# The low part of every second weight piece: an accumulating DMA in place of a VectorE subtraction

## The chip, the cores and the metric

The kernel runs on one core of one Trainium2 chip. The metric is device time in microseconds (us). Three runs of the kernel before took 2153.18, 2155.61 and 2155.78 us; their median is 2155.61 us.

## What is computed

Two layers of an encoder over 256 tokens of width 2048, in float32. Cut to what matters, a layer is

```
h   = RMSNorm(x);  p = h @ W_in                    # 2048 x 4624
A   = windowed attention;  M = mLSTM, both ways    # from the columns of p
x   = x + RMSNorm(concat(A, M) @ W_out)            # 2048 x 2048
x   = x + RMSNorm(relu(RMSNorm(x) @ W_up)^2 @ W_down)   # 2048 x 8192, 8192 x 2048
```

Nearly all the work is in the four products with the weights. The weights are 378 MB, read from HBM once.

## The kernel before

**Precision.** Each float32 operand of a product is split in two float32r parts: the high part is the operand rounded (written by ScalarE as a plain copy), the low part is the operand minus the high part. A product is then three matmuls: high by high, high by low, low by high. In the up projection the weights are the stationary operand and the moving operand holds both parts of the tokens, so two matmuls, of 512 and 256 columns, do the same.

**Tiles and pieces.** The weights are cut in column tiles, taken in the order of use: per layer 10 of the input projection (two of them narrow, 272 and 256 columns, the others 512), 4 of the output projection, and 4 blocks of 4 up tiles and 4 down tiles. That is 92 tiles in all. `load` (printed below) brings a tile in as four pieces q = 0..3, each [128, 4, 512] floats (1 MB), or [128, 16, 128] where the weights are stationary. For each piece SyncE's queue issues a DMA from `wall` in HBM to a buffer `raw` (L185), ScalarE writes the high part `whi` (L186), VectorE the low part `wlo` (L187). Of `raw` there are 2 buffers, of `whi` and `wlo` 4 each, all taken in turn. So the load of a piece waits until the piece two before it has been read out of `raw`, and the split of a piece waits until TensorE has ended with the piece four before it.

**Order.** `mm_tile` (L198 to L200 are its three matmuls) and `mm_stationary` (L266, L269) load their own tile and the one behind it, then issue the products. Work beside the products (attention, mLSTM, evacuation of PSUM) is emitted between them. Norms end on a chain over ScalarE (sums of squares, L309), VectorE and GpSimd (a power, L293 as `y_ro`, `y_rd`, `y_s`), then the residual (L788), transposes on TensorE (L328) and a split of the transposed tokens (`h2T`, `hT`: high part by ScalarE, L320, low part by GpSimd, L321). A scheduler sets each engine's order from a simulated time line. Each engine runs its own instructions in that order, so an instruction that waits holds up those behind it.

The first tile of all is loaded with a `begin` function in smaller steps; all others without.

Of the kernel before, what the change touches and what calls it, by code (L numbers as in the profile page):

```python
# [20 lines left out]
DM = 2048  # L21
# [22 lines left out]
# Column tiles of the input projection, in the order in which they are multiplied.  # L44
# [14 lines left out]
PK = 4  # contraction chunks in one weight piece  # L59
# [3 lines left out]
def _stage_widths():  # L63
    """Per layer: (stage, block, tile, width) in the order of use."""
    out = [("in", 0, j, w) for j, w in enumerate(IN_W)]
    out += [("out", 0, n, 512) for n in range(4)]
    for b in range(4):
        out += [("up", b, n, 512) for n in range(4)]
        out += [("down", b, n, 512) for n in range(4)]
    return out  # L70
# [5 lines left out]
def stationary(key):  # L76
    """Whether a column tile's weights are the stationary operand: the up projection's but for
    each layer's first, which starts on one token tile alone."""
    _, st, b, n = key
    return st == "up" and (b, n) != (0, 0)  # L80
# [6 lines left out]
def encoder_kernel(ctx, tc, x, wall, rope, conv_w, gate_bias, ml_g, sink, gpre, gpost, out):  # L87
# [14 lines left out]
    # ---------------------------------------------------------------- constants  # L102
# [15 lines left out]
    # column before row; column after row  # L118
# [24 lines left out]
    # rows split in two parts, the second NG2 further on, and what adds the two of one row  # L143
# [9 lines left out]
    # ---------------------------------------------------------------- weights  # L153
# [12 lines left out]
    def load(i, begin=None):  # L166
        """Load and split one column tile: four pieces, each [128, 4, w] of 512 rows, or, where
        the weights are stationary, [128, 16, 128] of 128 columns. begin(q) precedes piece q."""
        if i >= len(order) or order[i] in pieces:
            return  # L170
        o, w = offs[order[i]]
        k, n = (KC, P) if stationary(order[i]) else (PK, w)
        got = []
        for q in range(NPC):
            raw = wraw.tile([P, k, n], F32, tag="raw", name="raw")
            a = o + q * P * k * n
            src = wall[a:a + P * k * n].rearrange("(p k n) -> p k n", p=P, k=k)
            if begin is not None:
                begin(q)
            hi = wsp.tile([P, k, n], F32R, tag="hi", name="whi")  # L180
            lo = wsp.tile([P, k, n], F32R, tag="lo", name="wlo")
            step = 1 if begin is not None and q < 2 else k
            for j in range(0, k, step):
                sl = slice(j, j + step)
                nc.sync.dma_start(raw[:, sl], src[:, sl])  # L185
                nc.scalar.activation(hi[:, sl], raw[:, sl], AF.Copy)  # L186
                nc.vector.tensor_tensor(out=lo[:, sl], in0=raw[:, sl], in1=hi[:, sl].bitcast(F32), op=ALU.subtract)  # L187
            got.append((hi, lo))
        pieces[order[i]] = got
# [12 lines left out]
    # Work beside the products, emitted in small steps between them: `urgent` empties PSUM.  # L202
# [12 lines left out]
    def mm_tile(key, T, stages=(), after=None, at=None, half=False):  # L215
        """One column tile for both token tiles, in PSUM tiles for each. `stages`: (first, last)
        contraction chunks in which token tile 0 runs ahead of token tile 1; after(t, ps) is called
        behind each token tile's last product, at[t, k]() before a staged product. `half`: all work
        beside ends before the second half of the contraction."""
        load(pos[key])  # L220
        load(pos[key] + 1)
        if stages:
            ps = [psmm.tile([P, NT, 512], F32, tag="mm", name="mm")[:, 0] for _ in range(NT)]
        else:
            both = psmm.tile([P, NT, 512], F32, tag="mm", name="mm")
            ps = [both[:, t] for t in range(NT)]
        stages = list(stages)
        ended = []
        k = 0
        while k < KC:  # L230
            if stages and k == stages[0][0]:
                first, k = stages.pop(0)
                for t in range(NT):
                    for i in range(first, k):
                        if at is not None and (t, i) in at:
                            at[t, i]()
                        mm_k(ps[t], key, T, i, t)
                    if after is not None and k == KC:
                        after(t, ps[t])
                        ended.append(t)  # L240
                continue
            if half and k == KC // 2:
                while pump():
                    pass
            for t in range(NT):
                mm_k(ps[t], key, T, k, t)
            pump()
            k += 1
        if after is not None and not ended:
            for t in range(NT):  # L250
                after(t, ps[t])
        return ps

    def mm_stationary(key, T, after):
        """The transposed product of one column tile: weights stationary, both halves of the
        transposed tokens moving. after(pair, ps) gets two chunks of columns: [128, 2, 512] with
        the products of the tokens' upper and lower halves, to be added."""
# [15 lines left out]
    # ---------------------------------------------------------------- norms  # L273
    def rsq(ss, n, div, name):
        """(mean of squares + eps) ** -0.5 for n independent sums."""
# [12 lines left out]
    def rsq_row(part, last, name):  # L288
        """part: (sum of squares of the first columns) / DM + eps; last: the last columns' sum."""
# [33 lines left out]
    def pre(t, n, T, norm, eng=None):  # L323
        """512 columns of x of one token tile transposed, times the norm's gain, split."""
# [12 lines left out]
    def pre_scale(t, name):  # L337
        """The norm's scale of x of one token tile."""
        ss = small.tile([P, 4], F32, tag="ss", name=f"ss_{name}")
        for n in range(4):  # L340
            square_sum(xs[:, t, n * 512:(n + 1) * 512], ss[:, n:n + 1])
        return rsq_row(rsq_part(ss[:, :3], name), ss[:, 3:4], f"{name}{t}")

    # ---------------------------------------------------------------- attention
    def rope_half(ps, t, c0, nh, s):
        """Rotary on nh heads at columns c0.. of a product's tile; scaled by s."""
# [15 lines left out]
    SLACK = 3  # steps left for other engines  # L362
    ASC = float(HD) ** -0.5

    def attend(pair, qT, kT, vA, nsink, snk, attT):
        """Two heads of one group: heads 2*pair and 2*pair + 1."""
# [3 lines left out]
        for t in range(NT):  # L370
# [5 lines left out]
            # keys out of the window: beyond it for the first query tile, before it for the second  # L376
# [40 lines left out]
    # ---------------------------------------------------------------- mLSTM  # L417
    CF = 0.25 * float(HD) ** -0.5
    DIRS = ((0, 0, 1), (32, 1, 0))  # first row, first chunk, second chunk

    def gates(gp, cols):
        """gp [128, chunk, 16] -> rows of the scans, and columns in cols [128, 6, NG]:
        source exponents by chunk, end weights by chunk, floors by chunk."""
# [9 lines left out]
        # log1p(e) = 2 atanh(e / (2 + e)), by its series to beyond float32  # L433
# [41 lines left out]
        for r0, c1, c2 in DIRS:  # L475
# [4 lines left out]
            # running maximum behind the first chunk, in its own frame and in the next one's  # L480
# [23 lines left out]
    def conv_silu(zp, cw, dst):  # L504
        """Centred convolution over tokens and silu, times 2, of one chunk of channels."""
# [10 lines left out]
    def qk_heads(ps, c0, heads, s, cw, qk):  # L516
        """q and k columns of some heads from c0 on: transposed, convolved, activated."""
# [18 lines left out]
    def mlstm_head(h, qk, va, cols, hm, hr, name):  # L536
        """Both directions summed, into hm[:, h] [128, chunk, 256]; and its norm's scale, into hr."""
        # weights of sources for targets, transposed: [s, direction, t]
# [28 lines left out]
        # state behind each direction's first chunk, and q weighted for it  # L567
# [42 lines left out]
    def gate_in(h, ps, c0, sh, mg):  # L610
        """tanh of half of a head's gate; with it the sigmoid is (tanh + 1) / 2."""
        for t in range(NT):
            nc.scalar.activation(mg[:, h % 2, t], ps[t][:, c0:c0 + DV], AF.Tanh, scale=sh[t])

    def gate_mul(h, mg, hm, hr, gated):
        """A head normalised and gated, times 2."""
# [8 lines left out]
    def gate_out(h, hm, mlc, memT):  # L625
        """A gated head transposed, times its gain; split."""
# [11 lines left out]
    # ---------------------------------------------------------------- layers  # L638
# [16 lines left out]
    def pre_at(t, k, tp, T, norm):  # L655
        """Token tile tp's transposes within a staged tile, from token tile t's product k on."""
        return {(t, k + i): (lambda i=i: pre(tp, i, T, norm)) for i in range(4)}

    for l in range(DEPTH):
# [77 lines left out]
        # input projection  # L737
# [43 lines left out]
        # output projection, residual, next norm  # L781
# [37 lines left out]
        # MLP  # L819
# [87 lines left out]
def _pieces(w, cols=None):  # L907
    """[K, n] -> contiguous pieces [K / 512][128, 4, n], flat."""
# [47 lines left out]
```

## Time and profile before

| | |
|---|---|
| median of three runs | 2155.61 us |
| span of the profiled execution, first to last instruction | 2154.7 us |
| TensorE busy | 2118.5 us, 98% of the span |
| VectorE busy | 1211.4 us, 56% |
| ScalarE busy | 939.4 us, 44% |
| GpSimd busy | 60.9 us, 3% |
| moved by DMA | 388.13 MB, 51% of the 16 DMA engines' time |

The profiled execution has no time beside its span. The span lies 0.9 us under the median of the runs, inside their spread of 2.6 us. Busy time counts each engine by itself; that they overlap is read from the waits and the time line. TensorE's granted clock was 0.997 of its full 2.4 GHz.

### The profile page before, as it was taken

The numbers are of one execution on the slowest core, as the hardware profiler recorded it, in microseconds if no ns is written. First come the engines' busy times: TensorE is split into PE (matmuls) and PEld (weight loads), VectorE is DVE, ScalarE is ACT, GpSimd is POOL, SyncE is SP. The second block draws the span as 40 slices with busy tenths as digits, with TensorE's granted clock in tenths as the row PEclk, the third lists the DMA queues.
The fourth block names the chain that finished last, engine by engine and source line by source line (L and its number), as shares of the span: only waits on it lengthen the run. The fifth ranks groups of instructions, "written<-read, shape, count | busy, mean of one in ns | idle before, by whom it ended". The sixth has DMA issues, their size and how long they took to land.

```text
span 2154.7 us, 25194 instructions
## 1 busy us (share of the span) xinstructions
PE 2118.5 (98%) x10492; PEld 1779.7 (83%) x10492; DVE 1211.4 (56%) x1339; ACT 939.4 (44%) x1017; POOL 60.9 (3%) x68
## 2 busy tenths in 40 slices
PE   8999999999999999999999999999999999999998
PEld 6878887888888888888878788878888888888886
DVE  6656566654554555555576656565445545545554
ACT  5445545443443343344354554454434434433432
POOL 0000002000000000000020000030000000000000
PEclk9999999999999999999999999999999999999999
DMA  7434354555555555555554344546555555555553
GB/s 250 165 137 176 120 198 171 195 195 187 184 193 188 187 194 183 188 195 186 181 181 156 134 153 149 203 149 213 187 188 193 184 190 193 184 189 194 186 192 116
DMA packets 62195, 388.13 MB, mean 180 GB/s; under 512 B 9600, under 2 KB 10112, under 8 KB 17280
## 3 DMA queue, kind: packets, MB, share of 16 engines
q1 hardware_dynamic: 61936, 386.48, 51.2%
q8 instruction: 82, 1.34, 0.2%
q14 instruction: 33, 0.27, 0.0%
q10 hardware_dynamic: 144, 0.03, 0.0%
HBM read 384.39 MB, written 2.10 MB: 179 GB/s over the span
## 4 chain that ended last, share of the span: by engine, by line
PE 94%; DVE 2%; DMA 2%; ACT 1%; POOL 1%; issue 1%; POOLq 0%; DVEq 0%; SPq 0%; ACTq 0%
PE mms L266 21%; PE mm L200 19%; PE mm L199 19%; PE mm L198 19%; PE mms L269 11%; DMA raw<-wall 1%; PE sc L374 1%; PE pn L590 1%; PE po L413 1%; DVE xs L788 1%; POOL h2T L321 1%; DVE wlo L187 0%; ACT whi L186 0%; PE cp L573 0%; PE pn L593 0%
## 5 line engine op out<-in xcount | busy, mean ns | idle before, releaser
L187 DVE TENSOR_TENSOR wlo<-raw,whi 128x2048 fp32r<-128x2048 f32 (+3 forms) x374 | 828.8, 2217 | 811.2 <-ACT whi L186 810.7
L186 ACT ACTIVATE whi<-raw 128x2048 fp32r<-128x2048 f32 (+3 forms) x374 | 692.9, 1853 | 984.0 <-PE mm L200 537.8
L266 PE MATMUL mms<-h2T,whi 128*128 128x512 f32 x1920 | 678.8, 397 | 0.0
L269 PE MATMUL mms<-h2T,wlo 128*128 128x256 f32 x1920 | 539.7, 281 | 0.0
L266 PEld LDWEIGHTS mms<-h2T,whi 128*128 128x128 f32 x1920 | 361.0, 188 | 88.9
L200 PE MATMUL mm<-whi,uT 128*128 128x512 f32 x1024 | 403.1, 394 | 0.0
L199 PE MATMUL mm<-wlo,uT 128*128 128x512 f32 x1024 | 401.4, 392 | 0.0
L198 PE MATMUL mm<-whi,uT 128*128 128x512 f32 x1024 | 397.4, 388 | 0.0
L269 PEld LDWEIGHTS mms<-h2T,wlo 128*128 128x128 f32 x1920 | 360.4, 188 | 0.3
L198 PE MATMUL mm<-whi,hT 128*128 128x512 f32 (+2 forms) x640 | 241.8, 378 | 7.2 <-ACT hT L320 5.1
L200 PE MATMUL mm<-whi,hT 128*128 128x512 f32 (+2 forms) x640 | 241.6, 378 | 1.5 <-POOL hT L321 1.4
L199 PE MATMUL mm<-wlo,hT 128*128 128x512 f32 (+2 forms) x640 | 240.7, 376 | 0.0
L199 PEld LDWEIGHTS mm<-wlo,uT 128*128 128x128 f32 x1024 | 192.2, 188 | 44.7
L198 PEld LDWEIGHTS mm<-whi,uT 128*128 128x128 f32 x1024 | 192.2, 188 | 43.0
L200 PEld LDWEIGHTS mm<-whi,uT 128*128 128x128 f32 x1024 | 192.5, 188 | 38.3
L198 PEld LDWEIGHTS mm<-whi,hT 128*128 128x128 f32 x640 | 121.1, 189 | 28.0 <-ACT hT L320 5.7
L200 PEld LDWEIGHTS mm<-whi,hT 128*128 128x128 f32 x640 | 121.1, 189 | 23.2 <-POOL hT L321 2.2
L199 PEld LDWEIGHTS mm<-wlo,hT 128*128 128x128 f32 x640 | 121.0, 189 | 20.3 <-DVE wlo L187 0.2
L866 DVE SCALAR_TENSOR_TENSOR A_mlp<-mm,s2q,A_mlp 128x512 f32<-128x512 f32 x48 | 34.0, 746 | 37.9 <-PE mm L200 37.9
L198 PE MATMUL mm<-whi,memT 128*128 128x512 f32 x128 | 50.9, 398 | 0.0
L199 PE MATMUL mm<-wlo,attT 128*128 128x512 f32 x128 | 50.7, 396 | 0.0
L198 PE MATMUL mm<-whi,attT 128*128 128x512 f32 x128 | 50.6, 395 | 0.0
(220 smaller groups left out, 1403.4 us busy)
## 6 DMA issues: line engine op xcount, KB each, us to landing
raw<-wall SPq DMA_DIRECT2D x350, 1024.0 KB, 4.8
raw<-wall SPq DMA_DIRECT2D x8, 544.0 KB, 3.6
g<-gpost SPq DMA_DIRECT2D x16, 256.0 KB, 4.3
raw<-wall SPq DMA_DIRECT2D x8, 512.0 KB, 3.4
xs<-x_in SPq DMA_DIRECT2D x8, 256.0 KB, 5.3
raw<-wall SPq DMA_DIRECT2D x8, 256.0 KB, 6.7
y_out<-xs SPq DMA_DIRECT2D x8, 256.0 KB, 2.8
cossin<-rope SPq DMA_DIRECT2D x1, 256.0 KB, 7.7
```

Source lines behind the costliest of these rows:

```text
L186: nc.scalar.activation(hi[:, sl], raw[:, sl], AF.Copy)
L187: nc.vector.tensor_tensor(out=lo[:, sl], in0=raw[:, sl], in1=hi[:, sl].bitcast(F32), op=ALU.subtract)
L198: nc.tensor.matmul(dst, lhsT=xh, rhs=hi, start=(k == 0), stop=False)
L199: nc.tensor.matmul(dst, lhsT=xh, rhs=lo, start=False, stop=False)
L200: nc.tensor.matmul(dst, lhsT=xl, rhs=hi, start=False, stop=(k == KC - 1))
L266: nc.tensor.matmul(ps[:, i], lhsT=hi[:, k], rhs=Tk.rearrange("p j t -> p (j t)"), start=(k == 0), stop=False)
L269: nc.tensor.matmul(ps[:, i, :SEQ], lhsT=lo[:, k], rhs=Tk[:, 0], start=False, stop=(k == KC - 1))
L321: (eng or nc.vector).tensor_tensor(out=lo, in0=ps, in1=hi.bitcast(F32), op=ALU.subtract)
L374: nc.tensor.matmul(sc[:, j], lhsT=qT[:, q0 + j, t * P:(t + 1) * P], rhs=kT[:, g], start=(j == 0), stop=False)
L413: nc.tensor.matmul(po[:, j], lhsT=vA[:, kb, g * HD:(g + 1) * HD], rhs=pT[:, kb], start=(kb == 0), stop=(kb == 1))
L590: nc.tensor.matmul(pn[:, :DV + 1], lhsT=dt[:, d, c], rhs=va[:, c, h], start=True, stop=(c == c1))
L866: nc.vector.scalar_tensor_tensor(out=acc[:, t, sl], in0=ps, scalar=s2[t], in1=acc[:, t, sl], op0=ALU.mult, op1=ALU.add)
```

## The change

In every tile but the first, the pieces q = 1 and q = 3 are formed in another way. ScalarE writes minus the high part into `wlo` (a copy with scale -1). GpSimd's queue then issues a DMA that reads the same piece of `wall` from HBM once more and adds it onto `wlo`. ScalarE writes the high part into `whi` as before. VectorE has no part in these pieces. Nothing else changes; in the rest of the diff comments are taken out.

```diff
             for j in range(0, k, step):
                 sl = slice(j, j + step)
                 nc.sync.dma_start(raw[:, sl], src[:, sl])
+                if begin is None and q % 2 == 1:
+                    nc.scalar.activation(lo[:, sl], raw[:, sl], AF.Copy, scale=-1.0)
+                    nc.gpsimd.dma_start(lo[:, sl], src[:, sl], accum_op=ALU.add)
+                    nc.scalar.activation(hi[:, sl], raw[:, sl], AF.Copy)
+                    continue
                 nc.scalar.activation(hi[:, sl], raw[:, sl], AF.Copy)
                 nc.vector.tensor_tensor(out=lo[:, sl], in0=raw[:, sl], in1=hi[:, sl].bitcast(F32), op=ALU.subtract)
```

That concerns 182 pieces: 174 of 1 MB, 4 of 544 KB and 4 of 512 KB (the narrow tiles). In the changed kernel the lines behind the new ones stand 5 further on; L187 is minus the high part, L188 the DMA, L189 the high part of an odd piece, L191 and L192 the split of an even one.

ScalarE's order in the first down block of layer 0, before (`A_mlp` is the block's sum, which ScalarE writes behind each tile of this block; `uz` and `uT` are the up projection's evacuation and split in the block behind it):

```order
L186 ACTIVATE whi<-raw 128x2048 x4
L864 ACTIVATE A_mlp<-mm,s2q 128x512 x2
L186 ACTIVATE whi<-raw 128x2048 x4
L864 ACTIVATE A_mlp<-mm,s2q 128x512 x2
L186 ACTIVATE whi<-raw 128x2048 x2
L844 ACTIVATE uz<-mms 128x512
```

and at the same place in the changed kernel:

```order
L869 ACTIVATE A_mlp<-mm,s2q 128x512 x2
L191 ACTIVATE whi<-raw 128x2048
L187 ACTIVATE wlo<-raw 128x2048
L189 ACTIVATE whi<-raw 128x2048
L191 ACTIVATE whi<-raw 128x2048
L187 ACTIVATE wlo<-raw 128x2048
L189 ACTIVATE whi<-raw 128x2048
L869 ACTIVATE A_mlp<-mm,s2q 128x512 x2
L191 ACTIVATE whi<-raw 128x2048
L189 ACTIVATE whi<-raw 128x2048
L187 ACTIVATE wlo<-raw 128x2048
L849 ACTIVATE uz<-mms 128x512
```

Every second piece has two ScalarE instructions that read `raw`; in the down tiles minus the high part comes first, in the up tiles second.

GpSimd's order from the output projection to the first up tile of layer 0, before:

```order
L293 TENSOR_TENSOR y_ro_2869<-v_ro_2867,nhalf 128x1
L321 TENSOR_TENSOR h2T_2877<-xg,h2T_2877 128x4x128 x2
L321 TENSOR_TENSOR h2T_2878<-xg,h2T_2878 128x4x128 x2
L293 TENSOR_TENSOR y_ro_2959<-v_ro_2957,nhalf 128x1
```

and there in the changed kernel:

```order
L188 DMA wlo<-wall 128x2048 x6
L298 TENSOR_TENSOR y_ro_2897<-v_ro_2895,nhalf 128x1
L188 DMA wlo<-wall 128x2048
L298 TENSOR_TENSOR y_ro_2987<-v_ro_2985,nhalf 128x1
L326 TENSOR_TENSOR h2T_2905<-xg,h2T_2905 128x4x128
L188 DMA wlo<-wall 128x2048
L298 TENSOR_TENSOR y_s_3204<-v_s_3202,nhalf 128x1
L326 TENSOR_TENSOR h2T_2905<-xg,h2T_2905 128x4x128
L326 TENSOR_TENSOR h2T_2906<-xg,h2T_2906 128x4x128 x2
```

The power for the second token tile (`y_ro`) now stands ahead of the token split, and an accumulating DMA stands between the first and the second of the four splits of token tile 0.

## Rows read from the trace of the kernel before

**Rows 1.** The page's first part: busy time, share, instructions of each engine.
```profile
PE 2118.5 (98%) x10492; PEld 1779.7 (83%) x10492; DVE 1211.4 (56%) x1339; ACT 939.4 (44%) x1017; POOL 60.9 (3%) x68
```

**Rows 2.** The chain that ended last, shares of the span by engine.
```profile
PE 94%; DVE 2%; DMA 2%; ACT 1%; POOL 1%; issue 1%; POOLq 0%; DVEq 0%; SPq 0%; ACTq 0%
```

**Rows 3.** Busy time by stage: start:end, length, then engines, clock, DMA share, GB/s.
```profile
340.00:380.00 40.00, 37.96 (x183) 30.71 (x182) 28.49 (x50) 23.05 (x38) 16.38 (x12) 1.00 0.40 145
380.00:1060.00 680.00, 680.00 (x3413) 574.36 (x3412) 360.04 (x244) 276.22 (x206) 0.00 (x0) 1.00 0.54 191
1060.00:1100.00 40.00, 35.93 (x166) 29.04 (x165) 30.70 (x56) 19.55 (x33) 15.26 (x13) 0.96 0.42 145
...
1400.00:1450.00 50.00, 47.99 (x228) 39.13 (x227) 35.31 (x54) 27.41 (x42) 16.39 (x12) 1.00 0.40 140
```

**Rows 4.** Who waited for VectorE's low parts (line L187): total us, times.
```profile
  PEld mm L199: 0.9, 3
```

**Rows 5.** Groups by line and shape: count, busy us, mean ns, idle before.
```profile
L187 DVE TENSOR_TENSOR wlo<-raw,whi 128x2048 fp32r<-128x2048 f32 x350 | 803.3, 2295 | 783.4 <-ACT whi L186 783.2
...
L186 ACT ACTIVATE whi<-raw 128x2048 fp32r<-128x2048 f32 x350 | 670.7, 1916 | 941.5 <-PE mm L200 508.4 <-PE mms L266 366.4 <-DMA raw<-wall 61.9
...
L187 DVE TENSOR_TENSOR wlo<-raw,whi 128x1088 fp32r<-128x1088 f32 x8 | 10.3, 1290 | 13.3 <-ACT whi L186 13.3
...
L186 ACT ACTIVATE whi<-raw 128x1088 fp32r<-128x1088 f32 x8 | 8.9, 1114 | 19.4 <-PE mm L200 8.0 <-issue 7.4 <-DVE ra L359 2.4
```

**Rows 6.** ScalarE's time line, up tiles: start us, us, what, idle before and releaser.
```profile
604.39 1.92 ACT L186 ACTIVATE whi<-raw 128x2048 fp32r<-128x2048 f32 x1 [3.25 <-PE mms L266]
606.21 0.61 ACT L320 ACTIVATE uT<-uz 128x512 fp32r<-128x512 f32 x1
610.04 1.92 ACT L186 ACTIVATE whi<-raw 128x2048 fp32r<-128x2048 f32 x1 [3.22 <-PE mms L266]
```

**Rows 7.** ScalarE's time line, down tiles.
```profile
643.76 1.92 ACT L186 ACTIVATE whi<-raw 128x2048 fp32r<-128x2048 f32 x1 [3.06 <-PE mm L200]
649.26 1.92 ACT L186 ACTIVATE whi<-raw 128x2048 fp32r<-128x2048 f32 x1 [3.58 <-PE mm L200]
654.75 1.92 ACT L186 ACTIVATE whi<-raw 128x2048 fp32r<-128x2048 f32 x1 [3.58 <-PE mm L200]
```

**Rows 8.** VectorE's time line there.
```profile
645.72 2.29 DVE L187 TENSOR_TENSOR wlo<-raw,whi 128x2048 fp32r<-128x2048 f32 x1 [2.60 <-ACT whi L186]
```

**Rows 9.** DMA by window 600 to 626 us, 40 slices: busy tenths, GB/s.
```profile
DMA  9920009799700093799600075999301094999000
GB/s 429 416 88 0 0 0 176 239 441 441 315 0 0 0 139 63 328 416 403 265 0 0 0 101 151 403 403 403 151 0 25 0 176 164 441 429 391 13 0 0
```

**Rows 10.** DMA issues, window 400 to 1060 us: count, KB, median us to landing.
```profile
raw<-wall SPq DMA_DIRECT2D x120, 1024.0 KB, 4.8
```

**Rows 11.** DMA queue and issues, window 5 to 35 us.
```profile
q1 hardware_dynamic: 6324, 8.62, 87.4%
...
raw<-wall SPq DMA_DIRECT2D x4, 1024.0 KB, 7.4
```

**Rows 12.** The chain in window 340 to 380 us: start us, us, what.
```profile
351.17 2.29 DVE wlo L187
353.48 5.09 DMA raw<-wall
358.66 0.41 ACT whi L186
```

**Rows 13.** TensorE's time line in a narrow tile.
```profile
99.77 0.28 PE L198 MATMUL mm<-whi,hT 128*128 128x272 f32 x1
99.89 0.29 PE L199 MATMUL mm<-wlo,hT 128*128 128x272 f32 x1
```

**Rows 14.** GpSimd's time line at the border to the MLP.
```profile
357.35 2.56 POOL L321 TENSOR_TENSOR h2T<-xg,h2T 128x512 fp32r<-128x512 f32 x2 [9.51 <-ACT h2T L320]
361.17 4.14 POOL L321 TENSOR_TENSOR h2T<-xg,h2T 128x512 fp32r<-128x512 f32 x2 [1.25 <-ACT h2T L320]
```

## The prediction, on record before the changed kernel ran

> **What bounds the kernel now.** I read the page's busy times first: TensorE works 2118.5 us of a span of 2154.7 us, VectorE 56%, ScalarE 44%, GpSimd 3% [rows 1]. The chain that ended last puts 94% of the span on TensorE and 2% on VectorE [rows 2]. So next to nothing is to be had from VectorE's time as such. The table by stage says where TensorE waits at all: not at all in the long MLP stretch (680.00 us of 680.00), and 2.04, 4.07 and 2.01 us at the three borders between stages, 8.1 us together [rows 3]. All that TensorE waited for a low part is 0.9 us [rows 4].
>
> Then I looked at how the weights keep ahead. In the MLP a piece is split the moment TensorE lets go of the piece four before it (ScalarE's idle time ends on TensorE) [rows 6, 7]. Two pieces take 2 x 5.65 = 11.30 us in the up tiles (610.04 - 604.39) and 654.75 - 643.76 = 10.99 us in the down tiles. One buffer of `raw` is used once in that time: 4.8 us from issue to landing [rows 10], 1.92 us high part [rows 7], 2.29 us low part [rows 8], together 9.0 us. The margin of this loop is 2.0 us in the down tiles. It is the narrowest resource after TensorE. The DMA engines work 0.54 of the time [rows 3], in bursts: the busy tenths of a 26 us window show some 2.6 us of 9s and 7s for a piece, and as much rest [rows 9].
>
> **What goes and what comes.** VectorE loses 174 x 2.295 + 8 x 1.29 = 410 us [rows 5], hidden beside TensorE. Worth: between 0 and the 0.9 us of waits; I take 0.
>
> ScalarE gains 174 x 1.916 + 8 x 1.114 = 342 us [rows 5] (the four narrowest pieces are priced at the row of the next wider ones). In a pair of pieces it then has 3 x 1.92 and, in the up tiles, up to 2 x 0.61 us of other work [rows 6], 7.0 of 11.30 us. It is not the bound. The odd piece's `raw` is now free after two ScalarE instructions, 3.84 us, where it was 1.92 + 2.29 = 4.21; a gain of 0.4 us in that loop.
>
> GpSimd gains 182 DMA issues. No row shows one from its queue; hidden by 97% idle time, they matter only where something is queued behind, at the borders (below).
>
> The DMA engines get 182 transfers more. Cost of one: a copy of 1 MB takes 0.54 x 11.30 / 2 = 3.05 us of all engines [rows 3, 6], and 1.0486 MB at the best slices' 441 GB/s 2.38 us [rows 9]. An accumulating one reads the piece, reads `wlo`, and writes. Lower end: one copy, 3.05 us, since the same bytes come from HBM; a gain is excluded, for nothing is taken off the queues. Upper end: three copies, 9.15 us, if the three follow each other. I take two copies, two reads with the write beside the second; that is nearest to how a plain copy, one read with its write beside it, is priced in the row. Then a pair asks for 4 x 3.05 = 12.2 us of the engines by their mean cost, or 4 x 2.38 = 9.5 us at the best rate, of 10.99 to 11.30. So the engines are nearly full, and plain loads will land later.
>
> The Trainium skill, DMA: Bandwidth & Descriptors, section on issuing engines not being separate DMA queues, says that DMAs issued from GpSimd run on the same 16 engines as SyncE's and interleave with them; this speaks against the change, and by it the new transfers cannot pass beside the loads. The Trainium skill, Collectives: The Full Stack, part 3 on the bandwidth ceiling, has a reducing transfer at half a copy's rate (32.35 against 62.28 GB/s) because the add needs two source reads; by that one transfer is 1.93 x 3.05 = 5.9 us, an estimate, and a pair 12.0 us. No run here shows either yet.
>
> What crowding does to a load the trace shows at its start: with the engines at 87.4%, 1 MB took 7.4 us to land instead of 4.8 [rows 10, 11]. The odd piece's next load is issued just when the accumulating transfer starts, so it gets the crowded value; the even one's comes 5.65 us later and mostly not. With 0.1 us for the hand-overs (0.02 from VectorE to the issue, 0.09 from landing to ScalarE) [rows 12] the odd loop takes 7.4 + 3.84 + 0.1 = 11.34 us. That is 0.35 us over the down tiles' pair and 0.04 over the up tiles'. The pairs are 60 in the stationary up tiles, 114 in the other wide tiles (57 tiles, the first left out), 8 in the narrow ones. So 114 x 0.35 + 60 x 0.04 = 42 us. Ends: 0, if loads land within 7.0 us; and if the engines are the bound at 12.2 us, 114 x 1.21 + 60 x 0.90 = 192 us.
>
> Narrow tiles: their products follow at 0.12 us [rows 13], 24 to a piece, 2.95 us, a pair in 5.9. Behind each of the four such tiles two wide pairs come at 11.34, and 2 x 5.4 = 10.9 us of lead are used up. The low part of an odd piece had 3 x 5.5 = 16.5 us between its buffer coming free and its use; 3.84 of ScalarE and 7.4 or more of transfer leave some 5. At worst 6 to 8 us of waiting each, 32 in all; but the narrow pieces load in half the time, and the trace shows no wait there before. Between 0 and 32 us I take 3 each, 12.
>
> Borders: ahead of three of the four token splits of token tile 0 stands an accumulating DMA that waits for minus the high part of the up tile's last piece, and this for the last product of the output projection's. Before, those splits ran at 357 to 365 us as soon as ScalarE was ready [rows 14]. At the three borders I take one ScalarE instruction each, 1.92, together 6 us. Ends: 0, and 3 x (1.92 + 4.8) = 20 us, if GpSimd is held for as long as a load takes.
>
> Sum against the profiled span: 42 + 12 + 6 = 60 us on 2154.7. The median of the runs lies 0.9 us above the span, so 2155.6 + 60 = 2216 us, 2.8% slower.
>
> **The rivals.** First, the accumulating transfer costs about one copy: 9.2 us of the engines per pair, loads land soon after 4.8 us, the odd loop is 8.7 to 10 us and hides under TensorE; then 2156 us, at most 4 more from the borders. For it: the rests in the bursts, 2.6 us per piece [rows 9], hold just one such transfer. Against it: two sources.
>
> Second, it costs three copies or more: a pair needs 5 x 2.38 = 11.9 to 5 x 3.05 = 15.2 us, every odd low part comes late and TensorE waits for it everywhere. The price is 140 to 723 us, 2296 to 2880, the middle 2590. For it: nothing in this trace bounds an adding transfer from above. Against it: the bytes alone ask for two.
>
> Third, on the other side: at the borders VectorE's low part of 2.29 us stands in the chain ahead of the next load [rows 12]; without it norms and residuals end sooner and TensorE waits less. It decides if transfers cost one copy and GpSimd's splits aren't held. At most 8.1 + 0.9 us [rows 3, 4], 2147; at half of it 2151. Against it: ScalarE's added instructions stand in the same chain.
>
> That the change does not do what it says I rule out: the order shows the DMAs and VectorE's instructions gone.
>
> **How the numbers follow.** About 0.2%, 4.3 us, is what a measurement of this kernel tells from no change. Forecast (slower by waits at odd pieces, two copies) 0.52, with its own range 2162 to 2360; one copy 0.24; three copies 0.15; faster 0.09. That gives faster 0.09, same 0.24, slower 0.67. The range 2150 to 2420 us leaves out most of the faster case and two thirds of the three-copies case, 0.19.
>
> **What would show it.** Right: TensorE waits for `wlo` from the DMA, spread over the MLP, more in down than in up tiles; 1 MB loads landing at 7 us or later; DMA share near 0.9 or above with HBM bytes up by 187 MB; VectorE's group L192 at half its count. The first rival would show a DMA share near 0.8, loads near 5 us and TensorE still without a wait in the MLP. The second would show an accumulating transfer of over 9 us and pairs well over 12 us. The third would show the three borders shorter. The forecast is wrong in its main term if the time is lost at the borders or narrow tiles, or if TensorE's waits end on GpSimd's queue and not on transfers.

## The result, and the profile after

The changed kernel takes 2418.67 us (median of four runs, 2415.33 to 2431.04) against 2154.76 us before (four runs, 2153.18 to 2155.78): 1.1231 times as long, 95% interval 1.1213 to 1.1249. It is 264 us slower. The forecast was 60 us slower, with a range of its own up to 2360 us, which the time exceeds; it lies at the far end of the wide range, 2150 to 2420.

The page's first part (busy us, share of the span of 2419.2 us, instructions) and its DMA queues (packets, MB, share of 16 engines):

```profile
PE 2199.1 (91%) x10492; PEld 1813.5 (75%) x10492; DVE 814.0 (34%) x1157; ACT 1246.2 (52%) x1199; POOL 206.6 (9%) x250
...
q1 hardware_dynamic: 61936, 386.48, 41.7%
q0 software_dynamic: 26208, 186.79, 40.9%
...
HBM read 571.17 MB, written 2.10 MB: 237 GB/s over the span
```

Beside [rows 1], TensorE does the same instructions in 80.6 us more (2199.1 - 2118.5), and it idles 220.1 us instead of 36.2, which is 183.9 more. Up to 64 of the 80.6 us are the clock: it was granted 0.971 of 2.4 GHz in the mean instead of 0.997, so more products ran at the 1.2 GHz level. An estimate from the two means: 2 x 0.029 x 2419 = 140 us at the lower level instead of 2 x 0.003 x 2155 = 13, which costs at most half of the difference, 64 us; the rest was not taken apart. The table below has the clock lowest where TensorE waits most. VectorE lost 397 us of work and nothing came of it.

By stage (columns as in [rows 3]), the input projection and the MLP of layer 0:

```profile
40.00:380.00 340.00, 316.16 (x1488) 260.01 (x1488) 132.28 (x290) 186.82 (x253) 24.51 (x29) 0.97 0.79 225
...
430.00:1180.00 750.00, 689.47 (x3332) 570.84 (x3332) 212.18 (x175) 371.11 (x258) 51.52 (x60) 0.98 0.87 249
1180.00:1230.00 50.00, 38.85 (x159) 30.56 (x158) 26.45 (x49) 28.75 (x41) 11.33 (x13) 0.86 0.79 225
```

The MLP, where TensorE did not wait at all before, now has it idle 60.5 us in 750, with the DMA engines at 0.87 instead of 0.54. TensorE's first product of each stage, read from its time line, gives the length of the stages:

| stage | before, us | after, us | more |
|---|---|---|---|
| input projections, layers 0 and 1 | 257.5, 251.2 | 275.5, 266.1 | 18, 15 |
| output projections | 93.7, 93.7 | 110.2, 110.9 | 16, 17 |
| MLPs (layer 1: to the end) | 722.9, 728.1 | 824.7, 824.3 | 102, 96 |

Three quarters of the loss, 198 of 264 us, lie in the MLPs. What TensorE waited for in the whole execution (engine, line, waited for: us in all, times, longest us), then ScalarE; below, the same waits for down tiles (`uT`) and up tiles (`mms`), with the idle time behind the second bar:

```profile
PE mm L204 <- DMA wlo<-wall: 86.5, 51, 4.3
PE mms L274 <- DMA wlo<-wall: 73.0, 32, 4.8
...
ACT wlo L187 <- DMA raw<-wall: 562.3, 103, 8.2
```

```profile
L204 PE MATMUL mm<-wlo,uT 128*128 128x512 f32 x1024 | 410.6, 401 | 54.9 <-DMA wlo<-wall 54.8
L274 PE MATMUL mms<-h2T,wlo 128*128 128x256 f32 x1920 | 553.3, 288 | 73.0 <-DMA wlo<-wall 73.0
```

TensorE waits 159.5 us for accumulated low parts, 54.8 of them in the down tiles and 73.0 in the up tiles; in [rows 4] it waited 0.9 us for low parts. ScalarE, whose idle time ended on TensorE before [rows 5], now waits for loads: the weights no longer keep ahead. The DMA issues of the MLP (window 430 to 1180 us; count, KB, median us to landing) show how slow they became:

```profile
raw<-wall SPq DMA_DIRECT2D x119, 1024.0 KB, 8.0
wlo<-wall POOLq DMA_DIRECT2D x60, 1024.0 KB, 10.9
```

A load lands 8.0 us after its issue instead of 4.8 [rows 10]. In 750 us there are 59.5 pairs of loads, 12.6 us for a pair, where before it took 11.0 to 11.3 us [rows 6, 7]. One turn of the odd load buffer, in ScalarE's time line in down tiles (start us, us, what, idle before and releaser):

```profile
716.77 1.91 ACT L187 ACTIVATE wlo<-raw 128x2048 fp32r<-128x2048 f32 x1 [2.23 <-DMA raw<-wall]
718.59 1.90 ACT L189 ACTIVATE whi<-raw 128x2048 fp32r<-128x2048 f32 x1
727.79 1.92 ACT L191 ACTIVATE whi<-raw 128x2048 fp32r<-128x2048 f32 x1 [7.30 <-DMA raw<-wall]
732.79 1.92 ACT L187 ACTIVATE wlo<-raw 128x2048 fp32r<-128x2048 f32 x1 [3.08 <-DMA raw<-wall]
```

The accumulating transfer of this piece is issued at 719.1 us, the buffer's next load at 720.5, as soon as the high part is written. The load and the transfer run side by side and land nearly together, after 12.2 and 12.3 us:

```profile
L185 SPq DMA_DIRECT2D raw<-wall x1: 327/327/327, 720.5 to 720.5; - x1
...
DMA to landing us min/median/max: 12.2/12.2/12.2
```

From L187 to the next L187 are 16.0 us: 12.2 of landing and 3.8 of ScalarE. This is one of the worst turns. Of the 60 odd loads of this window the middle one landed after 9.0 us (mean 8.6, longest 12.4), of the even ones after 7.3 (mean 7.6). Read turn by turn, from one issue of the odd buffer's load to the next pass 12.65 us in the mean: 8.6 of landing, 0.3 until ScalarE reads the buffer, 3.7 for its two instructions. In 51 of the 60 turns ScalarE reads within 0.3 us of the landing, so this loop has no slack; the even buffer lies 0.8 us in the mean before it is read.

### The profile page after: what moved, and what is told of

Its sections match the earlier page's. It is cut to its first block, busy times and chain, and to the rows that moved or that the text cites. A ratio compares the mean times of both kernels' runs of the same rounds, so it can differ in the third digit from the quotient of the medians.

```text
span 2419.2 us, 25594 instructions
## 1 busy us (share of the span) xinstructions
PE 2199.1 (91%) x10492; PEld 1813.5 (75%) x10492; DVE 814.0 (34%) x1157; ACT 1246.2 (52%) x1199; POOL 206.6 (9%) x250
## 3 DMA queue, kind: packets, MB, share of 16 engines
q1 hardware_dynamic: 61936, 386.48, 41.7%
q0 software_dynamic: 26208, 186.79, 40.9%
## 4 chain that ended last, share of the span: by engine, by line
issue 39%; DMA 28%; PE 23%; ACT 6%; POOL 2%; DVE 1%; POOLq 0%; SPq 0%; ACTq 0%; DVEq 0%
DMA raw<-wall 15%; DMA wlo<-wall 13%; PE mms L271 5%; PE mm L204 4%; PE mm L205 4%; PE mm L203 4%; ACT wlo L187 3%; PE mms L274 2%; ACT whi L189 2%; POOL wlo L188 2%; DVE wlo L192 0%; PE pn L595 0%; ACT whi L191 0%; PE sc L379 0%; PE po L418 0%
## 5 line engine op out<-in xcount | busy, mean ns | idle before, releaser
L192 DVE TENSOR_TENSOR wlo<-raw,whi 128x2048 fp32r<-128x2048 f32 (+1 forms) x192 | 419.0, 2183 | 923.0 <-ACT whi L191 922.7
L271 PE MATMUL mms<-h2T,whi 128*128 128x512 f32 x1920 | 700.3, 406 | 11.8 <-ACT ur L840 5.6
L187 ACT ACTIVATE wlo<-raw 128x2048 fp32r<-128x2048 f32 (+2 forms) x182 | 340.9, 1873 | 612.2 <-DMA raw<-wall 562.3
L274 PE MATMUL mms<-h2T,wlo 128*128 128x256 f32 x1920 | 553.3, 288 | 73.0 <-DMA wlo<-wall 73.0
L204 PE MATMUL mm<-wlo,uT 128*128 128x512 f32 x1024 | 410.6, 401 | 54.9 <-DMA wlo<-wall 54.8
L189 ACT ACTIVATE whi<-raw 128x2048 fp32r<-128x2048 f32 (+2 forms) x182 | 339.7, 1866 | 227.7 <-DMA raw<-wall 156.7
L191 ACT ACTIVATE whi<-raw 128x2048 fp32r<-128x2048 f32 (+1 forms) x192 | 349.6, 1821 | 201.1 <-DMA raw<-wall 146.0
L271 PEld LDWEIGHTS mms<-h2T,whi 128*128 128x128 f32 x1920 | 371.3, 193 | 105.5 <-DVE uz L850 7.7
L274 PEld LDWEIGHTS mms<-h2T,wlo 128*128 128x128 f32 x1920 | 370.8, 193 | 84.1 <-DMA wlo<-wall 83.5
L188 POOL DMA_DIRECT2D wlo<-wall x182 | 157.2, 864 | 2050.3 <-ACT wlo L187 1961.5
L850 DVE TENSOR_TENSOR uz<-mms,uz 128x512 f32<-128x512 f32 x60 | 41.5, 691 | 331.3 <-ACT uz L849 321.4
L204 PEld LDWEIGHTS mm<-wlo,hT 128*128 128x128 f32 x640 | 123.4, 193 | 34.2 <-DMA wlo<-wall 13.2
```

What stands on the lines that cost most here:

```text
L187: nc.scalar.activation(lo[:, sl], raw[:, sl], AF.Copy, scale=-1.0)
L188: nc.gpsimd.dma_start(lo[:, sl], src[:, sl], accum_op=ALU.add)
L204: nc.tensor.matmul(dst, lhsT=xh, rhs=lo, start=False, stop=False)
L271: nc.tensor.matmul(ps[:, i], lhsT=hi[:, k], rhs=Tk.rearrange("p j t -> p (j t)"), start=(k == 0), stop=False)
L274: nc.tensor.matmul(ps[:, i, :SEQ], lhsT=lo[:, k], rhs=Tk[:, 0], start=False, stop=(k == KC - 1))
L850: nc.vector.tensor_tensor(out=z, in0=ps[:, :, :SEQ], in1=z, op=ALU.add)
```

## The experiments

Three explanations stood against each other. The load loop (T1): loads land late beside the accumulating transfers, and two load buffers, the odd one held for two ScalarE instructions after that, cannot turn fast enough. The late low part (T2): the accumulated low part itself comes too late for TensorE. Full engines (T3): the DMA engines simply have more work than time. Each kernel is the changed one with one edit. The kernel before, timed beside them, took 2155.9 to 2157.3 us (medians); each time below is followed by its ratio to that, with the 95% interval in brackets.

### A third load buffer, and its control

```diff
-    wraw = ctx.enter_context(tc.tile_pool(name="wraw", bufs=2))
+    wraw = ctx.enter_context(tc.tile_pool(name="wraw", bufs=3))
...
-    f2k = ctx.enter_context(tc.tile_pool(name="f2k", bufs=8))
-    f1k = ctx.enter_context(tc.tile_pool(name="f1k", bufs=5))
+    f2k = ctx.enter_context(tc.tile_pool(name="f2k", bufs=5))
+    f1k = ctx.enter_context(tc.tile_pool(name="f1k", bufs=4))
```

> The changed kernel with 3 buffers for loaded weights instead of 2 (the scratch pools f2k and f1k made smaller to give the space, 8 to 5 and 5 to 4). Theory 1, the load loop: plain loads land in 7.9 us instead of 4.8, and with two buffers the next load starts only when one has been read out, so the loop of landing and splitting sets the pace; with a third buffer the time falls to 2160 to 2260 us and TensorE's wait for the accumulated low parts falls below a third of 160 us. Theory 2, the late low part: the accumulating transfer itself (9.5 us to landing) is late for TensorE whatever the loads do: 2380 us or more. Theory 3, full DMA engines: the 16 engines cannot carry more, their share goes from 0.83 to 0.9 and above at most: 2250 to 2400 us.

Measured: 2227.8 us (2225.78 to 2233.3), 1.0333 [1.0317, 1.0349]. With a buffer more, 191 of the 264 us come back. TensorE's waits and the MLP's row (window 430 to 1080 us):

```profile
PE mm L204 <- DMA wlo<-wall: 36.5, 17, 4.3
...
PE mms L274 <- DMA wlo<-wall: 8.1, 13, 0.9
```

```profile
430.00:1080.00 650.00, 641.17 (x3196) 537.79 (x3195) 205.12 (x168) 359.90 (x247) 49.33 (x58) 1.00 0.98 278
```

The same transfers land later still (8.9 us for loads and 11.9 for accumulating ones, medians of the run), TensorE waits little, and the engines run at 0.98 and 278 GB/s. So in the changed kernel, at 0.87, they were not the bound: T3 falls for it. T2 falls too, as far as the landing time of the low part by itself is meant.

The edit also shrinks two pools to make room. The control has the smaller pools and two load buffers:

> The changed kernel with the smaller scratch pools of the run with three load buffers, but two load buffers. If the gain of that run is the third buffer's, as theory 1 has it: 2410 to 2440 us. If the smaller pools by their other order were part of it: below 2390 us.

Measured: 2424.62 us (2417.94 to 2424.91), 1.1232 [1.1215, 1.1248]. The pools do nothing; the third buffer is what counts.

### The second read without the add, and without the transfer

```diff
-                    nc.gpsimd.dma_start(lo[:, sl], src[:, sl], accum_op=ALU.add)
+                    nc.gpsimd.dma_start(lo[:, sl], src[:, sl])
```

> The accumulating DMA is a plain one from the same queue, so the low part of these pieces is the weight itself (the output is not the reference's). Same bytes from HBM, same order, same waits; the read of the destination and the addition are gone. If the price is the second read in the DMA engines (theories 1 and 3): their share for this queue falls from 40.9% to about half that time, loads land within 6.5 us and the time falls to 2160 to 2220 us. If it is the queue itself, GpSimd's issue of 0.86 us or the mere presence of a second stream: 2350 us or more.

Measured: 2170.86 us (2170.22 to 2172.14), 1.0065 [1.0048, 1.0082]. The queues, and the issues of the run:

```profile
q1 hardware_dynamic: 61936, 386.48, 48.7%
q0 software_dynamic: 26208, 186.79, 24.4%
...
raw<-wall SPq DMA_DIRECT2D x350, 1024.0 KB, 5.0
wlo<-wall POOLq DMA_DIRECT2D x174, 1024.0 KB, 5.2
```

The same bytes from the same queue take 24.4% x 2169.5 / 186.79 = 2.83 us of all engines per MB. Accumulated they took 40.9% x 2419.2 / 186.79 = 5.30, which is 1.87 times as much. With plain transfers a load lands after 5.0 us, and 248 of the 264 us are gone though each odd piece is still read from HBM twice. It is the accumulation (reading `wlo` and adding to it) that makes the transfer dear, not the second reading of the weights; which of its two halves it is, no run parts.

```diff
-                    nc.gpsimd.dma_start(lo[:, sl], src[:, sl], accum_op=ALU.add)
```

> No accumulating DMA: the low part of the odd pieces stays minus the high part (the output is not the reference's). What is left of the change is ScalarE's 182 added copies and VectorE's 182 subtractions less. All three theories: 2148 to 2162 us, the time of before. If ScalarE's 340 us more cost by themselves: above 2170 us.

Measured: 2161.98 us (2158.77 to 2163.77, ten runs), 1.002 [1.0011, 1.003]. ScalarE's 340 us of added instructions and their order cost at most some 5 us. VectorE's relief, which is whole here, brings nothing:

```profile
PE 2118.8 (98%) x10492; PEld 1781.3 (83%) x10492; DVE 815.8 (38%) x1157; ACT 1256.9 (58%) x1199; POOL 50.4 (2%) x68
```

### TensorE does not read the accumulated part

```diff
-            got.append((hi, lo))
+            got.append((hi, hi if begin is None and q % 2 == 1 else lo))
```

> TensorE reads the high part in place of the accumulated low part of the odd pieces (the output is not the reference's), so nothing but the next use of the buffer waits for the accumulating transfers; their traffic stays. Theory 2 (late low parts): 2160 to 2200 us. Theories 1 and 3 (loads or engines set the pace): TensorE waits for high parts or VectorE's low parts instead, 2330 us or more.

Measured: 2483.34 us (2479.78 to 2486.99), 1.1513 [1.1496, 1.1531]. Nobody on TensorE waits for the accumulated part now, and the kernel is slower still. So the late low part (T2) is not the cause. TensorE's waits have moved to the high parts and to `uz`, the evacuation of the up tiles' products. In ScalarE's time line the odd buffer's loop stands bare:

```profile
PE mm L203 <- ACT whi L189: 87.3, 41, 5.6
PE mms L271 <- DVE uz L850: 62.6, 26, 8.1
```

```profile
655.93 1.92 ACT L187 ACTIVATE wlo<-raw 128x2048 fp32r<-128x2048 f32 x1 [5.82 <-DMA raw<-wall]
657.75 1.89 ACT L189 ACTIVATE whi<-raw 128x2048 fp32r<-128x2048 f32 x1
659.55 0.58 ACT L849 ACTIVATE uz<-mms 128x512 f32<-128x512 f32 x1
...
668.68 1.92 ACT L187 ACTIVATE wlo<-raw 128x2048 fp32r<-128x2048 f32 x1 [4.64 <-DMA raw<-wall]
...
682.51 1.92 ACT L187 ACTIVATE wlo<-raw 128x2048 fp32r<-128x2048 f32 x1 [5.70 <-DMA raw<-wall]
```

Two turns of 12.75 and 13.83 us. Over the window 430 to 1180 us the odd loads land after 9.0 us (median of 57, from 8.84 to 10.3; mean 9.25); 9.25 + 3.84 + 0.1 = 13.2 us is the prediction's loop with the mean landing, and 750 us with 115 loads, 57.5 pairs, are 13.0 us for a pair. In the changed kernel the same sum with its mean, 8.6 + 3.84 + 0.1 = 12.55, meets its 12.6 us. (The two ScalarE instructions overlap by 0.1 us and take 3.72 together; the sums are good to that.) Why a quarter of its odd loads land in under 6.4 us, and none here, is the next question. My guess was ScalarE's order: in all 182 odd pieces here minus the high part comes first, in the changed kernel in 126. Another clue is `uz`: ScalarE begins it behind the two instructions that wait for the load (L849 above), and TensorE's 62.6 us on it were 5.1 in the changed kernel; that was not tried.

### The high part first in the source

```diff
+                    nc.scalar.activation(hi[:, sl], raw[:, sl], AF.Copy)
                     nc.scalar.activation(lo[:, sl], raw[:, sl], AF.Copy, scale=-1.0)
                     nc.gpsimd.dma_start(lo[:, sl], src[:, sl], accum_op=ALU.add)
-                    nc.scalar.activation(hi[:, sl], raw[:, sl], AF.Copy)
```

> The changed kernel with the high part written ahead of minus the high part in the source, both still read from the loaded weights. The scheduler follows in part: minus the high part comes first at 100 odd pieces, where it was 126 in the changed kernel and 182 in the run with unread low parts. Where it comes first the accumulating transfer starts ahead of the next load. If the load is slowed more by a transfer that is already under way, the time goes with that number, as 2483 - 2418 = 65 us for 56 pieces says: 30 us less than the changed kernel, 2375 to 2400 us. If the order does not matter: 2410 to 2430 us.

Measured: 2415.27 us (2410.14 to 2418.05), 1.1203 [1.1187, 1.122]. The guess missed: minus the high part now comes first in only 100 pieces, and the time is that of the changed kernel within 4 us, as expected if the order does not matter. The count of pieces in one order or the other does not explain the 65 us by which the unread kernel is slower; that stays open.

### The load buffer freed one instruction earlier

Minus the high part is here written from the high part, so `raw` is free after one ScalarE instruction (1.92 us) instead of two.

```diff
-                    nc.scalar.activation(lo[:, sl], raw[:, sl], AF.Copy, scale=-1.0)
-                    nc.gpsimd.dma_start(lo[:, sl], src[:, sl], accum_op=ALU.add)
                     nc.scalar.activation(hi[:, sl], raw[:, sl], AF.Copy)
+                    nc.scalar.activation(lo[:, sl], hi[:, sl].bitcast(F32), AF.Copy, scale=-1.0)
+                    nc.gpsimd.dma_start(lo[:, sl], src[:, sl], accum_op=ALU.add)
```

> Two load buffers as in the changed kernel, but the odd pieces' high part is written first and minus the high part is read from it, not from the loaded weights: the load buffer comes free after one ScalarE instruction, 1.92 us, instead of two, and the accumulating DMA starts 1.9 us later against the next load. Theory 1 (the odd buffer's loop of landing, ScalarE and next load sets the pace at 12.6 us a pair): the loop shortens by 1.9 us or more, then the engines bind as with three buffers, 2220 to 2290 us, DMA share above 0.9. Theory 3 (engines already bind): 2390 us or more. Theory 2 (low parts late): they start later still, above 2420 us.

Measured: 2208.35 us (2206.15 to 2224.98), 1.0253 [1.0216, 1.029]. Work, bytes and buffers are the same, and 210 of the 264 us are back, more than expected. The input projection and the MLP by windows, the waits and the issues:

```profile
40.00:380.00 340.00, 318.61 (x1541) 264.89 (x1540) 143.84 (x312) 203.31 (x271) 29.14 (x35) 0.98 0.85 237
430.00:1080.00 650.00, 650.00 (x3253) 548.58 (x3252) 212.72 (x172) 367.58 (x250) 49.78 (x58) 1.00 0.99 283
```

```profile
PE mm L204 <- DMA wlo<-wall: 28.4, 17, 5.0
...
PE mms L274 <- DMA wlo<-wall: 1.5, 1, 1.5
```

```profile
raw<-wall SPq DMA_DIRECT2D x350, 1024.0 KB, 6.7
wlo<-wall POOLq DMA_DIRECT2D x174, 1024.0 KB, 10.0
```

In the middle of the MLP TensorE does not wait, though the engines stand at 0.99; of the 28.4 us, 5.6 lie in down tiles and the rest in the projections. The edit takes 1.9 us from the loop, and it also has the load issued a ScalarE instruction ahead of the accumulating transfer instead of behind it: the odd loads land after 7.2 us here (median of 57 from 430 to 1060 us), not 9.0. The loop is then 7.2 + 1.92 + 0.1 = 9.2 us, under the 11.0 of a pair, and in 55 of the 57 turns the landed load lies more than 0.3 us before ScalarE reads it (2.1 in the mean). Both causes act here, and this run does not part them. The tight loop is now the even buffer's: 6.7 us of landing, 4.2 of ScalarE and VectorE and 0.2 until it is read make 11.1, just the length of a pair. What is left, 53 us of the profiled span, is by stages 39 us in the input and output projections and 14 in the MLPs.

Both remedies together:

> Three load buffers and minus the high part read from the high part. With three buffers the engines were busy 0.98 of the time in the MLP, so a shorter loop should give nothing more: 2215 to 2235 us. If loads still bound there: below 2200 us.

Measured: 2205.56 us (2203.23 to 2208.57), 1.0225 [1.0208, 1.0242], the same as with the earlier release alone. A shorter hold leaves nothing for a third buffer to do, as one and the same loop would have it. The other way round it is not so: the time lies between the two ranges expected, and on top of the third buffer the earlier release still gave 22 us. Why, no run shows.

### Fewer accumulating transfers

Every fourth piece instead of every second, otherwise as in the changed kernel:

```diff
-                if begin is None and q % 2 == 1:
+                if begin is None and q == 3:
```

> Only the piece q = 3 of each tile is formed by the accumulating DMA, half as many. Theory 1: the odd buffer's loop is 12.6 us in every second round and 9 us in the others, mean 10.8 of 11.0 to 11.3, and the lead of the pieces carries the difference: 2156 to 2190 us. Engines: 0.55 + 0.25 of share, no bound. If each accumulating transfer costs by its own lateness: half of the loss stays, 2270 to 2300 us.

Measured: 2216.7 us (2212.08 to 2222.69), 1.0277 [1.0258, 1.0295]. Slower than I expected. The middle of the MLP keeps a little waiting with the DMA engines at 0.75:

```profile
430.00:1080.00 650.00, 641.57 (x3190) 540.28 (x3189) 267.58 (x197) 305.97 (x218) 24.94 (x29) 0.99 0.75 232
```

Transfers that leave a quarter of the engines' time free still make TensorE wait. The same with the earlier release:

> Minus the high part read from the high part, and only q = 3 formed by the accumulating DMA. The load buffer is held for one ScalarE instruction and the engines have 0.55 + 0.25 of share to carry, so neither the loop nor the engines bind: 2156 to 2172 us, where the same number of transfers with the load buffer held for two instructions took 2217. If half the transfers mean half of what was left (51 us) whatever else: 2180 to 2185 us.

Measured: 2189.4 us (2186.67 to 2195.05), 1.0167 [1.0148, 1.0186]. Not as expected either: half the transfers leave 34 of the 51 us that the earlier release with all of them left. The MLP and its end:

```profile
380.00:1080.00 700.00, 698.77 (x3496) 589.45 (x3495) 298.98 (x221) 339.46 (x245) 30.17 (x34) 1.00 0.77 234
1080.00:1130.00 50.00, 42.62 (x186) 33.95 (x185) 33.33 (x57) 28.52 (x40) 15.85 (x15) 0.93 0.55 175
```

The MLP is clean; what is lost is lost elsewhere. To see whether the projections alone hold it, the last kernel keeps the accumulating transfers (with the earlier release) in up and down tiles only:

```diff
-                if begin is None and q % 2 == 1:
+                if order[i][1] in ("up", "down") and q % 2 == 1:
```

> Minus the high part read from the high part, in the up and down tiles alone (128 of 182 pieces). With it everywhere TensorE did not wait in the MLP though the engines were busy 0.99 of the time, and the 51 us left lay in the input and output projections. If so: 2160 to 2178 us. If full engines cost in the MLP too, by the share of the pieces: 2190 us.

Measured: 2201.83 us (2197.2 to 2207.88), 1.0218 [1.0195, 1.024]. Not as expected: the projections are back at their old lengths (256.5 and 93.7 us in layer 0), but the MLPs now carry 22 and 20 us more than before. In layer 0 the windows show it at the entry:

```profile
358.00:420.00 62.00, 50.73 (x247) 41.99 (x246) 22.61 (x36) 37.43 (x43) 13.56 (x14) 0.94 0.77 226
420.00:1080.00 660.00, 659.32 (x3291) 555.93 (x3290) 216.43 (x180) 372.34 (x255) 50.78 (x59) 1.00 0.99 283
```

TensorE waits 11.3 us in the first 62 (2.0 before), with gaps of 4.84 and 4.04 us on low parts that land 10.8 and 12.7 us after their issue: here the late low part itself (T2) holds it up. In the last 24 us of this MLP it waits 9.4 (2.7 in 22 before). The middle of the MLP is clean once the loop is repaired, so the remaining 34 to 51 us lie about the borders and in the projections. They fall with the number of accumulating transfers, but less than in proportion: 51, 46 and 34 us for 182, 128 and 91. I take it that several pieces fall due at once there; that, and how it splits between landing, ScalarE and GpSimd, was not tried. No version beats the kernel before; without any added transfer there is already nothing gained, since TensorE is the bound there.

## Why the prediction was wrong

**Right.** The direction, and the mechanism: the odd load buffer's loop (landing, two ScalarE instructions, hand-over) as the resource that gives way, with TensorE waiting for `wlo` from the DMA all over the MLP. The accumulating transfer costs two copies: 5.30 us of the engines per MB beside 41.7% x 2419.2 / 386.48 = 2.61 for the plain loads of the same run, 2.03 times, and 1.87 times against plain transfers of its own queue. The Trainium skill, Collectives: The Full Stack, part 3 on the bandwidth ceiling, has ReduceScatter, whose add needs two source reads, at half of AllGather's rate (1.93 times); the ratio here, within one core, agrees. That the second read is the reason here is not shown. That the transfers of GpSimd's queue run on the loads' engines, as the Trainium skill, DMA: Bandwidth & Descriptors, section on issuing engines, has it, agrees with the loads' landing, 8.0 us instead of 4.8. HBM reads are up by 187 MB, VectorE's L192 stands at 192 of 374, and ScalarE's 340 us are hidden but for some 5 us at most. The rivals of one copy and of three copies fall by the same figures, though the range of the second, 2296 to 2880 us, holds the measured time, and its sign of over 9 us is met by the landing of an accumulating transfer (10.9 us in the MLP) but not by its cost, 5.30 x 1.0486 = 5.6 us for a piece. The third rival, on the other side, falls by the kernel without the transfer, which has all of VectorE's relief and is not faster.

**The step that failed** is "the odd piece's next load is issued just when the accumulating transfer starts, so it gets the crowded value". The crowded value was taken at 7.4 us, from a stretch where only plain loads stood beside each other [rows 11]. Beside an accumulating transfer it was 8.6 us in the mean and up to 12.4, and the even loads, taken to be mostly undisturbed, went to 7.6. In hindsight a bound was at hand in the prediction's own terms: a load that shares the engines with a transfer of two copies and lands with it has 4.8 us of its own [rows 10] and up to 2 x 2.38 to 2 x 3.05 us of the other, together 9.6 to 10.9; an estimate, with the measured mean between it and 7.4. The loop is then 12.55 us and not 11.34. As the loop sets the pace, that 1.2 us counts at every pair: against 10.99 the excess in the down tiles is 1.56 us instead of 0.35, against 11.30 in the up tiles 1.25 instead of 0.04. With the prediction's pairs that is 114 x 1.56 + 60 x 1.25 = 253 us instead of 42. An excess of 0.35 us was the difference of two sums, and the landing in one of them proved off by 1.2.

**The other terms.** The 253 us already come near the whole loss of 264. By stage they are 60 x 1.25 + 68 x 1.56 = 181 us in the MLPs and 46 x 1.56 = 72 in the projections; the stage table shows 198 and 67. The 12 us for narrow tiles and 6 for the borders were not measured apart. With the loop repaired, about 50 us are left, so they too were probably taken small; since the two losses overlap in the changed kernel, they cannot be added. (In the narrow tiles' sum, 24 x 0.12 is 2.88 and not 2.95, which changes nothing.) TensorE's slower clock was at nothing; whether it costs time of its own beside a loop that sets the pace, no run shows.

**Wrong in what would show it.** TensorE was to wait more in the down tiles than in the up tiles; it was the other way round, 54.8 us in the down tiles and 73.0 in the up tiles. The corrected sum, with more excess in the down tiles, does not give this either: it fits the total and not the split, which stays open. The DMA share was to be near 0.9; it was 0.87, and this is no sign of full engines, since the same transfers ran at 0.98 and 0.99 with the loop repaired. The upper end for full engines, 12.2 us for a pair, was too high as well: with the earlier release a pair fits into 11 us.

## What to carry to other kernels

Where a few buffers are refilled in a loop (landing, then the instructions that free them), price the loop with the landing time beside the transfer that starts at the same instant, and with a range for it: a margin smaller than the uncertainty of the landing is no margin. Engines that have time free on the average do not protect a load; here a share of 0.87 was a sign of a slow loop, and 0.99 ran without a wait. If traffic has to be added, first free the buffer early (one instruction less in the loop, with the load then issued ahead of the transfer, brought back 210 of 264 us), or give it a buffer more (191).

## What the runs showed of the hardware that was not expected

An accumulating transfer from HBM onto SBUF takes 1.87 times the engine time of a plain one of the same bytes, queue and shape (5.30 against 2.83 us per MB). It also takes longer to issue: GpSimd's busy time for one, from the groups of the changed kernel and of the one with plain transfers (mean ns behind the busy us), is 0.86 us instead of 0.54:

```profile
L188 POOL DMA_DIRECT2D wlo<-wall x182 | 157.2, 864 | 2050.3 <-ACT wlo L187 1961.5
```

```profile
L188 POOL DMA_DIRECT2D wlo<-wall x182 | 97.5, 536 | 1858.7 <-ACT wlo L187 1811.8 <-ACT cth L518 23.7 <-PE ptu L844 23.0
```

The granted clock fell where TensorE waited, down to 0.86 in the 50 us at the end of the MLP, of which it worked 38.85. Of the 264 us, 80.6 stand in the profile as busy time of TensorE, at most 64 of them by the clock; the prediction had not priced that.
